# The 32 stores of an instance normalisation go out through GpSimd instead of ScalarE

## The chip, the cores and the metric

The kernel runs on one core of a Trainium2 chip. The metric is the device time of one execution in microseconds (us); the time before is the median of three runs. Within the core, five engines run side by side, each with an instruction stream of its own: TensorE (PE), VectorE (DVE), ScalarE (ACT), GpSimd (POOL) and SyncE (SP). Three of them issue transfers here: SP, ScalarE and GpSimd. Each has a DMA queue of its own, and all queues are served by the same 16 DMA engines.

## The reference

The input x has the shape (4, 8, 16, 256, 256) in float32: 512 channels of 65,536 elements each. Every channel is normalised by its own mean and variance and scaled by one gamma:

```python
mu = x.mean(axis=(3, 4), keepdims=True)
var = ((x - mu) ** 2).mean(axis=(3, 4), keepdims=True)
x_norm = (x - mu) / np.sqrt(var + 1e-5)
out = x_norm * gamma[None, :, :, None, None]
```

So 134.2 MB are read, 134.2 MB are written, and little is computed on each element.

## The kernel before, in words

The work is cut into U = 32 tiles of 128 partitions by 8192 elements, 4 MB each. One channel lies on S = 8 neighbouring partitions, so a tile holds K = 16 channels. In memory a tile is one contiguous block, and a partition's row is 32 KB of it. There are AHEAD = 6 slots in SBUF, `xt0` to `xt5`; tile u uses slot u % 6, and is normalised in place, so that the slot is free for tile u + 6 only when the store of tile u has landed.

The order is written by hand (`manual_schedule`): every engine runs its instructions in the order in which the program names them, and waits are put in where data or a slot are needed. Before the loop, gamma's row of 512 B is loaded on GpSimd's queue (L52), and the first six tiles are loaded (L53 and L54, through the helper at L47 and L48): tiles 1 and 3 on ScalarE's queue, the others on SP's. GpSimd then writes the small constants, among them `navg`, a 128 x 128 block matrix that sums over the eight partitions of a channel and multiplies by -1/65536.

The loop at L100 does the following for each tile:

- L102, VectorE: the sum of each partition's row.
- L103, ScalarE: the sum of the squares of each row; the squares themselves go to a scrap tile.
- L111, TensorE: the matrix `navg` turns both columns into minus the mean and minus the mean square of the channel.
- L112, VectorE, and L116, ScalarE: minus the variance, and its root with 1e-5 added.
- L120 and L122, VectorE: the reciprocal, times gamma.
- L125, VectorE: the whole tile, minus the mean, times the scale, in place.
- L129: the store of the tile, issued by ScalarE.
- L131: the load of tile u + 6 into the slot, issued by SP, which waits for the store of tile u to land.

On ScalarE the order is therefore: squares of tile u (L103), root (L116), store (L129), squares of tile u + 1. The store waits for L125 of its tile, and the next squares stand behind it. On GpSimd nothing is left in the loop. Completion of transfers is counted on semaphores that are handed out in turn, eight for the transfers of SP and ScalarE together and eight for those of GpSimd; a transfer that gets a semaphore again waits until the former user of it has landed.

Of the kernel before, what the change touches and what calls it, by code (L numbers as in the profile page):

```python
# [1 line left out]

# [4 lines left out]

F32 = mybir.dt.float32
U8 = mybir.dt.uint8
ALU = mybir.AluOpType  # L10
ACTF = mybir.ActivationFunctionType
AX = mybir.AxisListType


@with_exitstack
def kernel(
    ctx: ExitStack,
    tc: tile.TileContext,
    x: bass.AP,
    gamma: bass.AP,  # L20
    out: bass.AP,
):
    nc = tc.nc
    B, G, C, H, W = x.shape
    P = nc.NUM_PARTITIONS
    HW = H * W
    n_ch = B * G * C
    S = 8
    K = P // S
    F = HW // S  # L30
    U = n_ch // K
    NG = (G * C) // K
    AHEAD = 6
    assert HW % S == 0 and (G * C) % K == 0

    xv = x.rearrange("b g c h w -> (b g c h w)").rearrange("(u p f) -> u p f", p=P, f=F)
    ov = out.rearrange("b g c h w -> (b g c h w)").rearrange("(u p f) -> u p f", p=P, f=F)
    gv = gamma.rearrange("g c -> (g c)")

    data = ctx.enter_context(tc.tile_pool(name="data", bufs=1))  # L40
    singles = ctx.enter_context(tc.tile_pool(name="singles", bufs=1))
    psum = ctx.enter_context(tc.tile_pool(name="psum", bufs=4, space=bass.MemoryType.PSUM))
    ctx.enter_context(tc.manual_schedule())

    slots = [data.tile([P, F], F32, name=f"xt{i}") for i in range(AHEAD)]

    def load(u, queue):  # L47
        queue.dma_start(out=slots[u % AHEAD][:], in_=xv[u])  # L48


    g_row = singles.tile([1, G * C], F32, name="g_row")
    nc.gpsimd.dma_start(out=g_row[:], in_=gv[None, :])  # L52
    for u in range(AHEAD):  # L53
        load(u, nc.scalar if u in (1, 3) else nc.sync)  # L54


    eps_t = singles.tile([P, 1], F32, name="eps_t")
    nc.gpsimd.memset(eps_t[:], 1e-5)  # L58
    one = singles.tile([1, 1], F32, name="one")
    nc.gpsimd.memset(one[:], 1.0)  # L60
    navg = singles.tile([P, K, S], F32, name="navg")
    nc.gpsimd.memset(navg[:], -1.0 / HW)  # L62
    nc.gpsimd.affine_select(  # L63
        out=navg[:], in_=navg[:], pattern=[[-S, K], [0, S]], compare_op=ALU.is_ge,
        fill=0.0, base=0, channel_multiplier=1,
    )
    nc.gpsimd.affine_select(  # L67
        out=navg[:], in_=navg[:], pattern=[[S, K], [0, S]], compare_op=ALU.is_ge,
        fill=0.0, base=S - 1, channel_multiplier=-1,
    )  # L70
    navg_w = navg[:].rearrange("p k s -> p (k s)")
    root_eps = singles.tile([P, 1], F32, name="root_eps")
    nc.scalar.activation(out=root_eps[:], in_=eps_t[:], func=ACTF.Sqrt)  # L73
    g_rep = singles.tile([1, NG, K, S], F32, name="g_rep")
    g_ps = psum.tile([P, NG], F32, name="g_ps", bufs=1)
    g_col = singles.tile([P, NG], F32, name="g_col")

    nc.vector.tensor_copy(  # L78
        out=g_rep[:],
        in_=g_row[:].rearrange("o (n k) -> o n k", n=NG).unsqueeze(3).to_broadcast([1, NG, K, S]),  # L80
    )
    for n in range(NG):
        nc.tensor.matmul(  # L83
            out=g_ps[:, n : n + 1],
            lhsT=g_rep[:, n].rearrange("o k s -> o (k s)"),
            rhs=one[:],
            start=True, stop=True,
        )
    nc.vector.tensor_copy(out=g_col[:], in_=g_ps[:])  # L89

    junk = singles.tile([P, F], U8, name="junk")

    st = singles.tile([P, U, 2], F32, name="st")
    nvar = singles.tile([P, U], F32, name="nvar")
    std = singles.tile([P, U], F32, name="std")
    rstd = singles.tile([P, U], F32, name="rstd")
    scale = singles.tile([P, U], F32, name="scale")

    squares = []
    for u in range(U):  # L100
        t = slots[u % AHEAD]
        nc.vector.reduce_sum(out=st[:, u, 0:1], in_=t[:], axis=AX.X)  # L102
        square = nc.scalar.activation(  # L103
            out=junk[:], in_=t[:], func=ACTF.Square, accum_out=st[:, u, 1:2],
        )
        if u:

            tc.declare_no_dep(square.ins, squares[-1].ins, reason="junk, ordered by the root between")
        squares.append(square)
        ps = psum.tile([P, 2], F32, name="ps")  # L110
        nc.tensor.matmul(out=ps[:], lhsT=navg_w, rhs=st[:, u], start=True, stop=True)  # L111
        nc.vector.tensor_scalar(  # L112
            out=nvar[:, u : u + 1], in0=ps[:, 0:1], scalar1=ps[:, 0:1],
            scalar2=ps[:, 1:2], op0=ALU.mult, op1=ALU.add,
        )
        nc.scalar.activation(  # L116
            out=std[:, u : u + 1], in_=nvar[:, u : u + 1], func=ACTF.Sqrt,
            bias=eps_t[:], scale=-1.0,
        )
        nc.vector.reciprocal(out=rstd[:, u : u + 1], in_=std[:, u : u + 1])  # L120
        g = u % NG
        nc.vector.tensor_mul(  # L122
            out=scale[:, u : u + 1], in0=rstd[:, u : u + 1], in1=g_col[:, g : g + 1],
        )
        nc.vector.tensor_scalar(  # L125
            out=t[:], in0=t[:], scalar1=ps[:, 0:1], scalar2=scale[:, u : u + 1],
            op0=ALU.add, op1=ALU.mult,
        )
        nc.scalar.dma_start(out=ov[u], in_=t[:])  # L129
        if u + AHEAD < U:  # L130
            load(u + AHEAD, nc.sync)  # L131


# [1 line left out]
_INS = ['x', 'gamma']  # L135
_OUTS = [((4, 8, 16, 256, 256), 'float32')]


# [23 lines left out]
```

## Time and profile before

| what | value |
|---|---|
| time, median of 3 runs (lowest to highest) | 627.16 us (626.78 to 627.45) |
| span of the profiled execution | 625.2 us |
| time around the span (median less span) | 1.96 us |
| VectorE busy | 443.2 us (71%) |
| ScalarE busy | 238.8 us (38%) |
| TensorE matmuls busy | 21.4 us (3%) |
| GpSimd busy | 1.9 us |
| moved by DMA, mean rate | 268.46 MB, 429 GB/s |

The span is that of one profiled execution, from its first to its last record; the profiled execution's own device time is not listed apart, so the median of the runs stands beside it. The page has one line for each engine that divides the span into 40 slices, and a digit in it is the busy share of a slice in tenths, 9 being 90% or more. A line of the groups names the source line, the engine, the operation, what it writes and reads, and how often it runs; behind the first bar stand the total busy time in us and the mean of one in ns, behind the second the idle time of the engine just before these instructions and what ended it. A line of the DMA queues has the packets, the MB and the share of the 16 engines' time. A line of the DMA issues has the size of one in KB and the median time from issue to landing in us. The chain of waits follows the work that ended last back to its start.

### The profile page before, as it was taken

The numbers are of one execution on the slowest core, as the hardware profiler recorded it, in microseconds if no ns is written. First come the engines' busy times: TensorE is split into PE (matmuls) and PEld (weight loads), VectorE is DVE, ScalarE is ACT, GpSimd is POOL, SyncE is SP. The second block draws the span as 40 slices with busy tenths as digits, with TensorE's granted clock in tenths as the row PEclk, the third lists the DMA queues.
The fourth block names the chain that finished last, engine by engine and source line by source line (L and its number), as shares of the span: only waits on it lengthen the run. The fifth ranks groups of instructions, "written<-read, shape, count | busy, mean of one in ns | idle before, by whom it ended". The sixth has DMA issues, their size and how long they took to land.

```text
span 625.2 us, 627 instructions
## 1 busy us (share of the span) xinstructions
PE 21.4 (3%) x80; PEld 19.6 (3%) x80; DVE 443.2 (71%) x162; ACT 238.8 (38%) x98; POOL 1.9 (0%) x10
## 2 busy tenths in 40 slices
PE   2000000000000000000000000000000000000000
PEld 2000000000000000000000000000000000000000
DVE  0588999999776687666786767867668676687730
ACT  0444444444443244432344423444224442244400
POOL 1000000000000000000000000000000000000000
DMA  8999999999999999999999999999999999999998
GB/s 369 436 403 436 436 436 436 436 426 432 434 434 436 424 434 436 436 434 436 436 421 434 434 434 432 432 434 436 436 434 436 436 419 434 434 436 432 432 434 369
DMA packets 9251, 268.46 MB, mean 429 GB/s; under 512 B 1057, under 2 KB 1057, under 8 KB 1057
## 3 DMA queue, kind: packets, MB, share of 16 engines
q10 hardware_dynamic: 4896, 142.61, 52.9%
q1 hardware_dynamic: 4320, 125.83, 46.8%
q14 instruction: 3, 0.02, 0.0%
q0 software_dynamic: 32, 0.00, 0.0%
HBM read 134.22 MB, written 134.22 MB: 429 GB/s over the span
## 4 chain that ended last, share of the span: by engine, by line
another core or an unknown queue 61%; DMA 17%; DVE 15%; SPq 1%; PE 1%; issue 0%; ACT 0%
DMA xt<-in_x_dram 10%; DVE st L102 10%; DMA out_dram<-xt 8%; DVE xt L125 5%; SPq L48 1%; PE ps L111 1%; ACT std L116 0%; DVE nvar L112 0%; DVE rstd L120 0%; DVE scale L122 0%
## 5 line engine op out<-in xcount | busy, mean ns | idle before, releaser
L102 DVE TENSOR_REDUCE st<-xt 128x1 f32<-128x8192 f32 x32 | 277.9, 8684 | 105.3 <-DMA xt<-in_x_dram 105.3
L103 ACT ACTIVATE junk<-xt 128x8192 uint8<-128x8192 f32 x32 | 224.9, 7029 | 275.4 <-DMA xt<-in_x_dram 232.2
L125 DVE TENSOR_SCALAR xt<-xt,ps,scale 128x8192 f32<-128x8192 f32 x32 | 145.6, 4550 | 1.2
L116 ACT ACTIVATE std<-nvar,eps_t 128x1 f32<-128x1 f32 x32 | 9.4, 294 | 79.7 <-DVE nvar L112 79.7
L111 PE MATMUL ps<-st,navg 128*128 128x2 f32 x64 | 17.9, 349 | 562.0 <-DVE st L102 562.0
L111 PEld LDWEIGHTS ps<-st,navg 128*128 128x128 f32 x64 | 16.1, 312 | 563.8 <-issue 563.8
L112 DVE TENSOR_SCALAR nvar<-ps 128x1 f32<-128x1 f32 x32 | 9.2, 287 | 23.9 <-PE ps L111 23.9
L120 DVE RECIPROCAL rstd<-std 128x1 f32<-128x1 f32 x32 | 5.3, 164 | 11.6 <-ACT std L116 11.6
L78 DVE COPY g_rep<-g_row 1x1024 f32<-1x1024 f32 x1 | 0.7, 683 | 10.6 <-DMA g_row<-in_gamma_dram 10.6
L103 ACT ACTIVATION_READ_ACCUMULATOR junk<-xt 128x1 f32 x32 | 6.0, 186 | 0.0
L122 DVE TENSOR_TENSOR scale<-rstd,g_col 128x1 f32<-128x1 f32 x32 | 5.1, 159 | 1.1
L83 PE MATMUL g_ps<-one,g_rep 1*128 1x1 f32 x16 | 3.5, 347 | 11.5 <-DVE g_rep L78 11.5
L83 PEld LDWEIGHTS g_ps<-one,g_rep 1*128 1x128 f32 x16 | 3.5, 326 | 11.4 <-issue 11.4
L89 DVE COPY g_col<-g_ps 128x8 f32<-128x8 f32 x1 | 0.2, 167 | 3.7 <-PE g_ps L83 3.7
L73 ACT ACT_TABLE_LOAD x1 | 1.3, 1283 | 1.7 <-PEq L146 1.7
L52 POOL DMA_DIRECT2D g_row<-in_gamma_dram x1 | 0.6, 607 | 0.8 <-POOLq L146 0.8
L63 POOL TENSOR_SCALAR_AFFINE_SELECT navg<-navg 128x128 f32<-128x128 f32 x1 | 0.4, 398 | 0.1
L67 POOL TENSOR_SCALAR_AFFINE_SELECT navg<-navg 128x128 f32<-128x128 f32 x1 | 0.4, 398 | 0.1
L62 POOL MEMSET navg<- 128x128 f32 x1 | 0.2, 230 | 0.0
L73 ACT ACTIVATE root_eps<-eps_t 128x1 f32<-128x1 f32 x1 | 0.2, 203 | 0.0
L58 POOL MEMSET eps_t<- 128x1 f32 x1 | 0.1, 118 | 0.0
L146 POOL MEMSET const-bfloat16-1.0<- 128x1 bf16 x1 | 0.1, 102 | 0.0
(4 smaller groups left out, 0.4 us busy)
## 6 DMA issues: line engine op xcount, KB each, us to landing
out_dram<-xt ACTq DMA_DIRECT2D x32, 4096.0 KB, 62.5
xt<-in_x_dram SPq DMA_DIRECT2D x30, 4096.0 KB, 38.5
xt<-in_x_dram ACTq DMA_DIRECT2D x2, 4096.0 KB, 31.8
g_row<-in_gamma_dram POOLq DMA_DIRECT2D x1, 0.5 KB, 9.3
```

Of the source, the lines that this page charges most:

```text
L48: queue.dma_start(out=slots[u % AHEAD][:], in_=xv[u])
L73: nc.scalar.activation(out=root_eps[:], in_=eps_t[:], func=ACTF.Sqrt)
L78: nc.vector.tensor_copy(out=g_rep[:], in_=g_row[:].rearrange("o (n k) -> o n k", n=NG).unsqueeze(3).to_broadcast([1, NG, K, S]),)
L83: nc.tensor.matmul(out=g_ps[:, n : n + 1], lhsT=g_rep[:, n].rearrange("o k s -> o (k s)"), rhs=one[:], start=True, stop=True,)
L102: nc.vector.reduce_sum(out=st[:, u, 0:1], in_=t[:], axis=AX.X)
L103: square = nc.scalar.activation(out=junk[:], in_=t[:], func=ACTF.Square, accum_out=st[:, u, 1:2],)
L111: nc.tensor.matmul(out=ps[:], lhsT=navg_w, rhs=st[:, u], start=True, stop=True)
L112: nc.vector.tensor_scalar(out=nvar[:, u : u + 1], in0=ps[:, 0:1], scalar1=ps[:, 0:1], scalar2=ps[:, 1:2], op0=ALU.mult, op1=ALU.add,)
L116: nc.scalar.activation(out=std[:, u : u + 1], in_=nvar[:, u : u + 1], func=ACTF.Sqrt, bias=eps_t[:], scale=-1.0,)
L120: nc.vector.reciprocal(out=rstd[:, u : u + 1], in_=std[:, u : u + 1])
L122: nc.vector.tensor_mul(out=scale[:, u : u + 1], in0=rstd[:, u : u + 1], in1=g_col[:, g : g + 1],)
L125: nc.vector.tensor_scalar(out=t[:], in0=t[:], scalar1=ps[:, 0:1], scalar2=scale[:, u : u + 1], op0=ALU.add, op1=ALU.mult,)
```

## The change

The store at L129 is issued by GpSimd, on GpSimd's own DMA queue, and no longer by ScalarE. All 32 stores move. Nothing else in the program's text changes: the loads, the order of VectorE, TensorE and SP, the slots and the arithmetic stay. Since the semaphores of GpSimd's transfers are a set of their own, loads and stores no longer share one set.

```diff
@@ -126,7 +126,7 @@
             out=t[:], in0=t[:], scalar1=ps[:, 0:1], scalar2=scale[:, u : u + 1],
             op0=ALU.add, op1=ALU.mult,
         )
-        nc.scalar.dma_start(out=ov[u], in_=t[:])
+        nc.gpsimd.dma_start(out=ov[u], in_=t[:])
         if u + AHEAD < U:
             load(u + AHEAD, nc.sync)
```

## The prediction

> **What bounds the kernel now.** I read the page's busy line and its DMA part first, because a kernel that reads and writes 134.2 MB each and computes little should be held by the transfers. From the page of before:
>
> ```profile
> span 625.2 us, 627 instructions
> ...
> DMA  8999999999999999999999999999999999999998
> ...
> q10 hardware_dynamic: 4896, 142.61, 52.9%
> q1 hardware_dynamic: 4320, 125.83, 46.8%
> ...
> q0 software_dynamic: 32, 0.00, 0.0%
> ```
>
> The 16 DMA engines are busy from wall to wall. Queue q1 is SP's (30 loads), q10 ScalarE's (32 stores and 2 loads), q0 GpSimd's (so far only gamma). The shares of the two large queues add up to 99.7%: 623.3 of 625.2 us. So at most 1.9 us of idle DMA time is left in the whole span. The trace's records of single packets say what fills it: 8192 packets of 32,768 bytes (64 DMAs x 128 rows), median 1213 ns. 8192 x 1.213 / 16 = 621.1 us. On each engine the two queues take turns, one packet of q1, then one of q10.
>
> Next I read the groups, to see whether an engine is near that bound.
>
> ```profile
> L102 DVE TENSOR_REDUCE st<-xt 128x1 f32<-128x8192 f32 x32 | 277.9, 8684 | 105.3 <-DMA xt<-in_x_dram 105.3
> L103 ACT ACTIVATE junk<-xt 128x8192 uint8<-128x8192 f32 x32 | 224.9, 7029 | 275.4 <-DMA xt<-in_x_dram 232.2
> L125 DVE TENSOR_SCALAR xt<-xt,ps,scale 128x8192 f32<-128x8192 f32 x32 | 145.6, 4550 | 1.2
> ```
>
> VectorE needs 8.68 + 4.55 + 1.8 for the small steps = 15.05 us a tile; a load and a store take 2 x 9.68 = 19.36 us. VectorE idles 4.35 us a tile on the load. Last, the DMA issues and the end of the chain of waits:
>
> ```profile
> out_dram<-xt ACTq DMA_DIRECT2D x32, 4096.0 KB, 62.5
> xt<-in_x_dram SPq DMA_DIRECT2D x30, 4096.0 KB, 38.5
> ...
> g_row<-in_gamma_dram POOLq DMA_DIRECT2D x1, 0.5 KB, 9.3
> ```
>
> ```profile
> 547.02 38.50 DMA xt<-in_x_dram
> 585.51 0.02 issue
> 585.54 8.70 DVE st L102
> ```
>
> A slot's round is 38.5 (load) + 15.05 (compute) + 62.5 (store) = 116.05 us = 6 slots x 19.36 = 116.2: a store spends 62.5 us on 9.68 us of moving, so the rest is backlog. The last load lands at 585.5, its store is issued at 600.6 and lands with the span's end at 625.2. Of those 24.6 us, 9.7 are its own; 14.9 us is backlog of earlier stores, **the cover of the end**.
>
> **The change, part by part.** Times are against this execution's 625.2 us; the median of the runs shown is 627.16, 1.96 us above it, and I carry that difference over.
>
> *Removed from ScalarE:* 32 DMA issues of 0.338 us = 10.8 us, with the wait of each on L125. ScalarE runs 224.9 + 9.4 + 6.0 us of 625 and idles 275.4 us before L103, of which 232.2 for a load. In the first eight tiles (43.2 us in all) L103 stood behind the store's wait on L125; now it can start earlier, but it takes 7.03 us beside a reduce of 8.68 that can't start earlier, since VectorE itself runs L125 then. Worth 0.
>
> *Added on GpSimd:* 32 issues. GpSimd's other work is 1.90 us, over before the first load lands at 22.8 us, so nothing stands behind a waiting store, and only the next store follows it. Loads on SP wait for the same event as before, the landing of store u. The instruction lists of both programs show SP, VectorE and TensorE in the same order. Semaphores change: a store used to wait for the store four tiles back (77 us earlier, 62.5 to land, so nobody waited); now it waits for that eight back. Worth 0.
>
> *Price of one issue:* the trace has one on this queue, gamma's, 0.607 us, with 32 packets. A store has 144 on its queue now (128 rows, and 16 packets of 4 B that signal the end). Lower bound 0.34 (as ScalarE), upper 0.607 x 144 / 32 = 2.73 us. I take 2.7, the row on the same engine. It delays a store by up to 2.4 us, inside 62.5 us of which 52.8 are backlog: 0 in the middle. At the end 2.4 of the 14.9 us of cover go: 0. Without that cover it would be 2.4 us once, not 32 times.
>
> *GpSimd's issuing beside VectorE.* No row shows an issue of GpSimd beside L125. L125 handles 8192 elements in 4.55 us, L102 the same 8192 in 8.68. A store is issued right after its L125 ends; then VectorE idles 4.35 us and reduces for 8.68, so the next L125 is at least 10.4 us off (8.68 + 1.8, in the first tiles). 2.7 us fit there, so I take 0. Bounds: no clash, or one whole L125, 4.55 us, for a store (backlog again: 0) or the other way 2.7 us for VectorE, inside its 4.35 us of idling. The Trainium skill speaks against this change here: "SBUF — State Buffer", "Who interferes with whom", says that a VectorE instruction in a two-port mode (tensor_scalar can be one, tensor_reduce can't) and a GpSimd instruction block each other until the first ends, and that a DMA issued by GpSimd is starved by it. L125's half time agrees with such a mode; that GpSimd is blocked, no run here shows yet. By that rule alone every store would be up to 4.55 us late, 146 us for 32 if nothing covered them.
>
> *The packets themselves* are the one price no row gives: a 32 KB row on q0. Gamma's 32 packets show that q0 takes turns like the others: its 9 ns packets stand between packets of q1 and q10, and the next packet starts 6 ns later, also after the signalling ones. So turns and signals cost nothing visible. Lower bound of the difference: nothing, 1213 ns is moving time; the whole idle rest, 625.2 - 621.1 = 4.1 us, can't become less than the start of the first load and the last landing, so a gain stays under 1 to 2 us. Upper bound: if rows are cut. The trace has 8192-byte packets of 307 ns; 4 x 307 = 1228, 15 ns above 1213, so about 5 ns a cut. Cut into 4 KB pieces: 7 x 5 to 7 x 9 (the 9 ns of a packet with no data) = 35 to 63 ns a row, x 4096 rows / 16 = 9 to 16 us. I take 0: all 8192 rows here went whole, and gamma's row came as 16 packets of 32 B, one per engine, and 16 of 4 B.
>
> *The end.* For 585.5 to 625.2 us only stores move, on one queue. If that queue had a gap per store, no load would fill it. Lower bound 0 (the 6 ns above); upper bound: the first packets of the kernel took about 1.9 us, 0.7 above 1213; four stores x 0.7 = 2.8 us. I take 0, the nearer row, and keep 2.8.
>
> Sum: 0. 625.2 + 1.96 = 627.2 us.
>
> **Rivals.**
> *A, no change to speak of*, 626.0 to 628.4.
> *B, q0 moves the same bytes at more cost*: rows cut, or gaps with nobody to fill them. For it: q0 has never carried a large row here, and with 99.7% busy every extra ns shows: 4.9 ns a row already make 1.25 us, the point from which it decides. Prices: 2.8 us from the end (630.0), 9 to 16 us for 4 KB pieces (636 to 643).
> *C, stores win the turns from the loads.* Then the last load lands late and the cover is gone. It decides once stores gain more than 14.9 us of moving on the loads, about 1.5 stores; at worst only the last store is left when its load lands, and the end is 15.05 + 9.7 us of bare work after 621.1 - 9.7 us of moving, plus the 4.1 idle: 640. Against it: turns are one packet each now. If the loads win instead, the backlog grows and nothing is lost.
> *D, faster*: store 0 no longer stands behind the two loads on q10, and is in motion some 4 us sooner, at 37.8 us instead of 42. But a full DMA only changes whose packet goes first. At best 1 to 2 us of idle and slow first packets vanish: 625.5.
> *E, the change doesn't act*: the changed program's list has all 32 stores on GpSimd, so it acts; if they still went by q10, 627.2.
>
> **How the numbers follow.** A measurement of this kernel can tell about 0.2% (1.25 us) from no change. A with E 0.50; B 0.35 (a third each near 630, at 636 to 643, and above); C 0.08; D 0.07. Same is A and E, 0.50; slower B and C, 0.43; faster D, 0.07. Predicted time 627.2; its own range 626.0 to 628.4. The 8-in-10 range goes from 625.6 to 641: it leaves out B's third above, the dearest 4 KB pieces and the best of D.
>
> **What would show it.** Right: q0 with 4608 packets and 134 MB and the stores' median time to landing near 60 us; 32 KB packets still near 1213 ns; DMA at 9 in all slices; VectorE still idle about 105 us before L102, L125 at 4550 ns; the last load landing near 585 us. B shows as more packets on q0 or longer ones, and a DMA share over 99% with a longer span, or as gaps in the last 40 us. C shows as shorter stores, longer loads, and a last load after 600 us. A clash with VectorE shows as L125 over 4550 ns or GpSimd issues of more than 4 us. I am wrong above all if a row costs more on this queue.

## The result, and the profile after

The change makes the kernel slower by 0.35%: 628.71 us (median of 8 runs, 628.09 to 632.55) against 627.15 (8 runs), a ratio of 1.0035 with a 95% interval of 1.0025 to 1.0045. The difference of the medians is 1.56 us. That lies in the forecast's range, above the own range of its likeliest case (626.0 to 628.4), and outside what counted there as no change.

The profiled execution of the change took 630.6 us, with a span of 628.6, more than most: six of the eight runs lie between 628.09 and 628.86, two at 630.6 and 632.55. So its trace shows 3.4 us of span more than before, where a usual run has some 1.6. Both have to be explained.

From the page of the change, the lines that answer to those shown of before, and that of the new GpSimd issues (L129):

```profile
span 628.6 us, 628 instructions
...
DMA  8999999999999999999999999999999999999996
...
q0 software_dynamic: 4640, 134.22, 49.5%
q1 hardware_dynamic: 4320, 125.83, 46.6%
q10 hardware_dynamic: 288, 8.39, 3.1%
...
L102 DVE TENSOR_REDUCE st<-xt 128x1 f32<-128x8192 f32 x32 | 277.9, 8683 | 106.4 <-DMA xt<-in_x_dram 106.4
L103 ACT ACTIVATE junk<-xt 128x8192 uint8<-128x8192 f32 x32 | 224.8, 7026 | 235.0 <-DMA xt<-in_x_dram 235.0
L125 DVE TENSOR_SCALAR xt<-xt,ps,scale 128x8192 f32<-128x8192 f32 x32 | 145.6, 4551 | 1.2
L116 ACT ACTIVATE std<-nvar,eps_t 128x1 f32<-128x1 f32 x32 | 9.4, 295 | 121.8 <-DVE nvar L112 121.8
...
L129 POOL DMA_DIRECT2D out_dram<-xt x32 | 17.0, 532 | 582.1 <-DVE xt L125 582.1
...
out_dram<-xt POOLq DMA_DIRECT2D x32, 4096.0 KB, 64.2
xt<-in_x_dram SPq DMA_DIRECT2D x30, 4096.0 KB, 36.4
```

The middle is as before. The stores are on q0 with 4640 - 32 = 4608 packets, rows whole. The trace's single packets of 32 KB have a median of 1213 ns on q0 as on q1. VectorE waits 106.4 us for loads (105.3 before), L125 takes 4551 ns (4550), and the DMA line has its nines. ScalarE's waits only changed their name: its wait on L125 (43.2 us before) is gone, and that of L116 on L112 grew from 79.7 to 121.8 us, by 42.1. What differs is the last digit of the DMA line: 6 after 8. The time went in at the end.

The end stands in the view of line 157, the barrier that closes the program. A line gives shortest, median and longest duration in ns, then the start of the first and of the last. Before:

```profile
L157 POOLq EVENT_SEMAPHORE  x4: 17/17/17, 624.4 to 625.1; - x4
L157 POOLq DRAIN  x3: 40/93/7988, 2.7 to 624.9; - x3
L157 SPq DRAIN  x3: 7/7/7, 624.3 to 624.6; - x3
```

After:

```profile
L157 POOLq EVENT_SEMAPHORE  x4: 17/17/17, 627.8 to 628.5; - x4
L157 POOLq DRAIN  x3: 46/108/25972, 601.8 to 628.3; - x3
L157 SPq DRAIN  x3: 7/7/7, 626.6 to 628.0; - x3
```

SP has seen the last store when its first drain starts, at 624.3 before and 626.6 after. Before, GpSimd is waiting by then and answers at 624.4; its long drain, 7.99 us from 2.7 us on, ended when gamma had landed. After, its drain starts behind the last issue at 601.8, takes 25.97 us and ends at 627.8, **1.2 us after SP knows that everything has landed**. All engines wait for it. By the trace's records of packets and instructions the 3.44 us divide so:

| stretch, us | before | after |
|---|---|---|
| start to first 32 KB packet | 1.81 | 1.82 |
| first to last packet | 622.08 | 624.23 |
| last packet to the end | 1.30 | 2.59 |

The last row is +1.29 us, close to the whole difference of the medians. The middle row, +2.15, is one DMA engine. The last store's last packets end within 0.85 us of each other on 15 engines, and 2.43 us later on the sixteenth. On that engine 26 store packets, one per tile, start right after the load's 4-byte signal and take 1275 to 1354 ns, 2.29 us more than 26 x 1213; on the other engines the signals of load and store follow each other. Before, all 16 end within 1 us.

### The profile page after: what moved, and what is told of

Its sections match the earlier page's. It is cut to its first block, busy times and chain, and to the rows that moved or that the text cites. A ratio compares the mean times of both kernels' runs of the same rounds, so it can differ in the third digit from the quotient of the medians.

```text
span 628.6 us, 628 instructions
## 1 busy us (share of the span) xinstructions
PE 21.4 (3%) x80; PEld 19.5 (3%) x80; DVE 443.2 (71%) x162; ACT 238.1 (38%) x98; POOL 18.9 (3%) x42
## 3 DMA queue, kind: packets, MB, share of 16 engines
q0 software_dynamic: 4640, 134.22, 49.5%
## 4 chain that ended last, share of the span: by engine, by line
another core or an unknown queue 52%; DMA 17%; DVE 15%; issue 10%; SPq 1%; PE 1%; ACT 0%; POOL 0%; POOLq 0%
DVE st L102 10%; DMA xt<-in_x_dram 9%; DMA out_dram<-xt 8%; DVE xt L125 5%; SPq L48 1%; PE ps L111 1%; ACT std L116 0%; DVE nvar L112 0%; POOL out_dram L129 0%; DVE rstd L120 0%; DVE scale L122 0%; POOLq L157 0%; POOLq L129 0%
## 5 line engine op out<-in xcount | busy, mean ns | idle before, releaser
L102 DVE TENSOR_REDUCE st<-xt 128x1 f32<-128x8192 f32 x32 | 277.9, 8683 | 106.4 <-DMA xt<-in_x_dram 106.4
L125 DVE TENSOR_SCALAR xt<-xt,ps,scale 128x8192 f32<-128x8192 f32 x32 | 145.6, 4551 | 1.2
L116 ACT ACTIVATE std<-nvar,eps_t 128x1 f32<-128x1 f32 x32 | 9.4, 295 | 121.8 <-DVE nvar L112 121.8
L129 POOL DMA_DIRECT2D out_dram<-xt x32 | 17.0, 532 | 582.1 <-DVE xt L125 582.1
L112 DVE TENSOR_SCALAR nvar<-ps 128x1 f32<-128x1 f32 x32 | 9.2, 288 | 23.8 <-PE ps L111 23.8
```

The lines of the kernel that those rows point to most:

```text
L112: nc.vector.tensor_scalar(out=nvar[:, u : u + 1], in0=ps[:, 0:1], scalar1=ps[:, 0:1], scalar2=ps[:, 1:2], op0=ALU.mult, op1=ALU.add,)
L116: nc.scalar.activation(out=std[:, u : u + 1], in_=nvar[:, u : u + 1], func=ACTF.Sqrt, bias=eps_t[:], scale=-1.0,)
L125: nc.vector.tensor_scalar(out=t[:], in0=t[:], scalar1=ps[:, 0:1], scalar2=scale[:, u : u + 1], op0=ALU.add, op1=ALU.mult,)
L129: nc.gpsimd.dma_start(out=ov[u], in_=t[:])
```

## The experiments

The theory: (a) GpSimd's drain at the end, (b) one engine out of step. The rival: a price on every store of the queue. Behind each median stand, in brackets, its ratio to the kernel before, timed beside it, and the 95% interval of the ratio.

**1. The last store by ScalarE.**

```diff
-        nc.gpsimd.dma_start(out=ov[u], in_=t[:])
+        (nc.scalar if u == U - 1 else nc.gpsimd).dma_start(out=ov[u], in_=t[:])
```

> Stores 0 to 30 go by GpSimd, the last one by ScalarE. Theory: the 1.6 us of the change have two parts. (a) After its last store GpSimd's drain at the end of the program ends at 627.8 us where the last store had landed at 626.6: 1.2 us, once per kernel, and nothing is left to hide it. (b) On one DMA engine of 16 the turns of loads and stores are out of step, and there the store packet that follows a load's 4-byte signal takes about 1300 instead of 1213 ns, once per tile, 2 us in all in the profiled execution. By (a) this kernel hides the drain behind the last store (9.7 us) and comes to 627.2 to 627.6 us, GpSimd's drain ending well before SP's last wait. Rival: GpSimd's queue costs the same little more on every store; 31 of 32 stores are still there, so 628.6 to 628.8 us.

Measured: 628.77 us (1.0036, 1.0023 to 1.005). That is the rival's number, but the experiment did not do what I meant: the last store, on a queue of its own, took turns with the GpSimd stores still under way, so the two queues ended together, GpSimd's last of all on the one late engine (its last packet 1.2 us after ScalarE's), and the drain was not hidden: 2.56 us from the last packet to the end. It tells nothing apart.

**2. Only the last store by GpSimd.**

```diff
-        nc.scalar.dma_start(out=ov[u], in_=t[:])
+        (nc.gpsimd if u == U - 1 else nc.scalar).dma_start(out=ov[u], in_=t[:])
```

> Only the last store goes by GpSimd, 31 by ScalarE. Theory: part (a) is there in full, since the drain doesn't depend on the number of stores: 1.2 us more than before, 628.3 to 628.5 us, with GpSimd's drain ending about 1.2 us after the last landing. Rival 1, a price per store on GpSimd's queue: 627.2 us. Rival 2, a drain whose time grows with the number of stores issued: under 0.1 us, 627.2 us.

Measured: 627.55 us (1.0009, 1.0000 to 1.0018) against 626.94, between all the theories. The drain ended 0.63 us after its queue's last packet, where the change has 1.74. So this time does depend on what the queue did before.

**3 and 4. All loads by SP, with stores by GpSimd (3) or ScalarE (4).** The edit is the same in both:

```diff
-        load(u, nc.scalar if u in (1, 3) else nc.sync)
+        load(u, nc.sync)
```

> Stores by GpSimd as in the change, and all loads by SP, so that only two queues are in use. The first store then begins in the middle of a load (37.9 us, 3.6 loads after the first byte), and on no engine do the signals of a load and a store follow each other. Theory (b): then on all 16 engines one store packet per tile takes about 85 ns longer, 26 tiles, 2.2 us; with (a) 630.4 to 630.8 us, and 16 packets near 1300 ns per tile. Rival (one engine is slower because of GpSimd's queue, whatever the order of turns): as the change, 628.5 to 628.9 us, one long packet per tile.

> As the kernel before (stores by ScalarE), but all loads by SP, so that here too the first store begins in the middle of a load. Theory (b), if it is a matter of turns and not of the queue that issues: 2.2 us more than before, 629.2 to 629.5 us, with 16 long store packets per tile. Rival, that only GpSimd's queue has it: 627.2 us and no long packets.

Measured: 628.75 us (1.0032, 1.0019 to 1.0045) for 3 and 627.5 us (1.0009, 1.0000 to 1.0018) for 4. My theory of turns falls: in 3 again one engine alone is late, with 26 long packets (2.4 us), not 16 engines; in 4 some ten engines have the signals apart, and no store packet behind a load's signal is long. The rival holds for 3, and a late engine shows only where GpSimd's queue carries the stores.

**5. The last eight stores by ScalarE**, to have GpSimd's drain over early.

```diff
-        nc.gpsimd.dma_start(out=ov[u], in_=t[:])
+        (nc.scalar if u >= U - 8 else nc.gpsimd).dma_start(out=ov[u], in_=t[:])
```

> Stores 0 to 23 by GpSimd, the last eight by ScalarE, so that GpSimd's last store lands more than 30 us before the end and its drain is over by then (sending only the very last store by ScalarE did not do that: in the last 25 us the two queues share the engines and end together). Theory (a), GpSimd's drain is the cost: 627.0 to 627.5 us, no slower than before by more than 0.1%. Rival, the cost lies in the packets of the 24 stores or on the one late engine: 628.2 to 628.6 us. In the profiled execution the late engine should be late by about 1.5 us (18 tiles of 26).

**6. Only the last four stores by GpSimd.**

```diff
-        nc.scalar.dma_start(out=ov[u], in_=t[:])
+        (nc.gpsimd if u >= U - 4 else nc.scalar).dma_start(out=ov[u], in_=t[:])
```

> Only the last four stores by GpSimd. In the change GpSimd's drain ended 1.7 us after the last packet of its queue; with one store there it ended 0.6 us after. Theory A, the drain takes longer the more stores it has issued in the whole program (36 ns each): 0.7 us after the last packet, 627.6 us. Theory B, it depends on how many stores are in flight when it starts (four in the change): 1.7 us after the last packet, 628.4 to 628.8 us.

Measured: 648.72 us (1.0353, 1.0327 to 1.0379) and 646.02 us (1.0302, 1.0287 to 1.0317). Both miss everything that was expected, by 17 to 20 us. From the timeline of the kernel with four GpSimd stores (start, duration, what; in brackets the idle time before and what ended it):

```profile
547.17 8.69 DVE L102 TENSOR_REDUCE st<-xt 128x1 f32<-128x8192 f32 x1 [4.36 <-DMA xt<-in_x_dram]
...
582.12 8.69 DVE L102 TENSOR_REDUCE st<-xt 128x1 f32<-128x8192 f32 x1 [19.92 <-DMA xt<-in_x_dram]
...
616.81 8.69 DVE L102 TENSOR_REDUCE st<-xt 128x1 f32<-128x8192 f32 x1 [19.67 <-DMA xt<-in_x_dram]
...
632.13 0.53 POOL L129 DMA_DIRECT2D out_dram<-xt  x1 [34.16 <-DVE xt L125]
```

The last two tiles wait 19.9 and 19.7 us for their loads, where 4.36 is usual. With the old stores on one queue, the new on a second and the loads on a third, the engines take turns among three, and loads get one turn in three instead of one in two: in the packets of this trace the load, the ScalarE store and the GpSimd store under way at that time end together, each spread over the same 3.7 us. The last load lands at 616.8 instead of 585.5 us, and the last store goes out at 632.1 with no backlog to cover it. This is the prediction's rival C, shown on a kernel that has two store queues at once; the change has one. For the drain they still tell something: in 5 it ended 105 us before the end, and from the last packet to the end it was 1.32 us, as before. In 6 it ended 0.59 us after its queue's last packet; but only the last of the four stores was still under way when it began, so 6 does not tell the number of stores from the number in flight, as it was meant to. Nor does any engine fall behind in 5, where 1.5 us was expected: the signals of a store lie within 1.2 us of each other on the 16 engines up to 449 us, where the change has 4.0 by then.

**7. The stores' issue put beside L125.** GpSimd waits for the scale of the next tile, then issues the store. The load into the slot moves along with it, and the last store follows the loop; both stand outside the lines shown:

```diff
+        if u:
+            nc.gpsimd.tensor_copy(out=gate[:, u : u + 1], in_=scale[:, u : u + 1])
+            nc.gpsimd.dma_start(out=ov[u - 1], in_=slots[(u - 1) % AHEAD][:])
         nc.vector.tensor_scalar(
...
-        nc.gpsimd.dma_start(out=ov[u], in_=t[:])
```

> The store of tile u is held back on GpSimd until the scale of tile u + 1 is ready (a one-column copy on GpSimd waits for it), so that GpSimd issues each store while VectorE runs L125 of the next tile. Theory from the skill's rule on the shared port: the issue of 0.53 us takes until L125 ends, 4 to 5 us, or L125 grows from 4.55 by the issue's 0.5 us. Rival: the two don't meet, 0.53 and 4.55 us stay. The time: a store leaves 15 to 19 us later, out of 43 us of backlog, so less than 1% more by either theory, plus up to 10 us at the end if the last stores have lost their cover.

Measured: 629.4 us (1.0044, 1.0026 to 1.0063). From its groups (L129 is the old L125, L128 the store) and its timeline:

```profile
L129 DVE TENSOR_SCALAR xt<-xt,ps,scale 128x8192 f32<-128x8192 f32 x32 | 145.6, 4551 | 1.2
L128 POOL DMA_DIRECT2D out_dram<-xt x31 | 137.4, 4433 | 1.2
```

```profile
301.32 4.55 DVE L129 TENSOR_SCALAR xt<-xt,ps,scale 128x8192 f32<-128x8192 f32 x1
301.35 0.18 POOL L127 COPY gate<-scale 128x1 f32<-128x1 f32 x1 [14.72 <-DVE scale L123]
301.58 4.41 POOL L128 DMA_DIRECT2D out_dram<-xt  x1
```

An issue that took 0.53 us in the change takes 4.41 here and ends at 305.99, 0.12 us after VectorE's instruction (305.87). VectorE loses nothing. The Trainium skill, "SBUF — State Buffer", "A bandwidth-pool intuition that's wrong (but worth ruling out)", says that a DMA of GpSimd beside a VectorE tensor_copy is blocked until VectorE's end and about 115 ns more: this run agrees, with a tensor_scalar. GpSimd's small copy, which starts 0.03 us after L129, was over in 0.18 us all the same; no run here says why. Yet the time is 0.7 us from the change's, though each of 31 issues lost 3.9 us: the backlog covers it. In this trace no engine was late (all 16 within 1.8 us), though 434 store packets on GpSimd's queue start right after a load's signal, some 16 for a tile: none takes more than 1215 ns. So following a signal is not by itself what makes a packet long. The drain was as in the change (1.87 us after the last packet).

**8 and 9. Two slots instead of six**, with the stores by GpSimd (8) or ScalarE (9).

```diff
-    AHEAD = 6
+    AHEAD = 2
...
-        load(u, nc.scalar if u in (1, 3) else nc.sync)
+        load(u, nc.scalar if u == 1 else nc.sync)
```

> The change with two slots instead of six, so that the backlog of stores which hid GpSimd's issue is gone: a slot's round is load, compute, store, with nothing in between. Theory (the issue of GpSimd is dearer, and only the backlog hid it): slower than the same kernel with ScalarE's stores by 0.5 (issue 0.53 against 0.34 us, and 0.3 us later after L125) to 2.4 us (the prediction's upper price) in each of 16 rounds, 8 to 38 us. Rival (the issue costs nothing even when uncovered): within 2 us of it.

> The kernel before with two slots instead of six, to be set beside the change with two slots. A round of a slot needs at least 9.7 + 15.05 + 9.7 us and two landings, near 38 us, against 38.7 us of DMA work for two tiles: 650 to 720 us. Theory: 8 to 38 us faster than the change with two slots; rival: within 2 us of it.

Measured: 754.8 us with GpSimd (748.7 to 759.4; 1.203 times the kernel before, 1.1965 to 1.2095), 761.6 with ScalarE (760.4 to 762.1; 1.2138, 1.2118 to 1.2158). The theory is wrong in size and sign: without the backlog GpSimd's stores come out 7 us, 0.9%, faster. The 650 to 720 us that I had for the kernel with ScalarE's stores is missed too, by 42 us. The issue lines, GpSimd first:

```profile
out_dram<-xt POOLq DMA_DIRECT2D x32, 4096.0 KB, 15.2
xt<-in_x_dram SPq DMA_DIRECT2D x31, 4096.0 KB, 15.3
```

```profile
out_dram<-xt ACTq DMA_DIRECT2D x32, 4096.0 KB, 16.1
xt<-in_x_dram SPq DMA_DIRECT2D x31, 4096.0 KB, 15.3
```

The store leaves 0.3 us after L125 here (0.03 with ScalarE), but lands 0.9 us sooner after that, in the median. Load and store of the two slots still overlap for part of their way, and how far is set by when each starts. That this overlap is the cause is only argued; it stays open.

**10 to 12. The drain by itself.** The kernel before with small loads of gamma by GpSimd at the start, which nothing uses (n = 31 in 10 and 11, 7 in 12); 11 and 12 also send the last store by GpSimd.

```diff
+    extra = singles.tile([1, n, 16], F32, name="extra")
+    for i in range(n):
+        nc.gpsimd.dma_start(out=extra[:, i], in_=gv[None, 0:16])
...
-        nc.scalar.dma_start(out=ov[u], in_=t[:])
+        (nc.gpsimd if u == U - 1 else nc.scalar).dma_start(out=ov[u], in_=t[:])
```

> The kernel before, its stores on ScalarE, plus 31 loads of 64 B of gamma by GpSimd at the start, which nothing uses. Theory: what the change costs at the end is GpSimd's drain, and it costs only where the queue's last transfer lands at the program's end; here it lands early, so 626.9 to 627.3 us, as before. Rival, every DMA of GpSimd costs a little wherever it is: 628 us and more.

> The same 31 small loads at the start, and the last store by GpSimd: 33 DMAs on its queue as in the change, but only one of them a store. So far the drain ended 0.6 us after its queue's last packet with 2 to 5 DMAs issued, and 1.7 to 1.9 us with 25 to 33, whether one or four were still in flight. Theory A, it depends on how many DMAs the queue was given: 1.7 us after the last packet, the end 2.6 us after it, 628.4 to 628.8 us. Theory B, it depends on the bytes or packets of the stores: 0.6 us and 1.7 us, 627.5 us as with the last store alone.

> Seven small loads at the start and the last store by GpSimd: 9 DMAs on its queue, so that all eight semaphores of the queue are used, as in the change. Theory A with a time that grows per DMA (0.04 us each): drain 0.9 us after the last packet, 627.7 us. Theory A with a step when the semaphores are used a second time: 1.7 us, 628.5 us. Theory B: 0.6 us, 627.5 us.

Measured: 628.08 us (1.0019, 1.001 to 1.0028), 629.51 us (1.0041, 1.0029 to 1.0054) and 628.24 us (1.0021, 1.0012 to 1.003), against 626.8. The small loads are not free, against my expectation, and 628.08 is what the rival had named: from first to last packet 622.98 us in 10, 0.9 more than before, of which their 62 packets on each engine are 0.56 at 9 ns. But 11 has the same 622.98, so the pair 10 and 11 isolates the end: 1.43 us in the medians, 1.45 in the traces. The closing barrier of 10 and then of 11:

```profile
L160 POOLq DRAIN  x3: 40/106/35072, 111.6 to 625.8; - x3
L160 SPq DRAIN  x3: 7/7/7, 625.2 to 625.5; - x3
```

```profile
L160 POOLq DRAIN  x3: 40/99/24961, 601.7 to 627.2; - x3
L160 SPq DRAIN  x3: 7/7/7, 625.5 to 626.9; - x3
```

In 10 the long drain is over at 146.7 us and nobody waits for it. In 11 it ends at 601.7 + 25.0 = 626.7, 1.2 us after SP is ready, as in the change, though one store alone went by GpSimd: the rival, a price on every store, is not needed for this. The drain's time after the last packet, 1.89 us in 11 and 0.91 in 12, is near what a time that grows with the number of DMAs had foretold (1.7 and 0.9); the times are longer than foretold (628.4 to 628.8 and 627.7), as the small loads cost something of their own. The traces whose last packets bear on it:

| kernel | DMAs given to GpSimd | queue's last packet to drain's end, us | last packet of all to the end, us |
|---|---|---|---|
| before | 1 | 0.42, early | 1.30 |
| last store only (2) | 2 | 0.63 | 1.70 |
| last four (6) | 5 | 0.59 | 1.74 |
| 7 small and the last (12) | 9 | 0.91 | 1.75 |
| first 24 (5) | 25 | 1.67 | 1.32 |
| 31 small (10) | 32 | 1.68, early | 1.29 |
| all but the last (1) | 32 | 1.71 | 2.56 |
| the change | 33 | 1.74 | 2.59 |
| two slots (8) | 33 | 1.73 | 2.58 |
| loads by SP (3) | 33 | 1.83 | 2.67 |
| beside L125 (7) | 33 | 1.87 | 2.71 |
| 31 small and the last (11) | 33 | 1.89 | 2.74 |

The third column rises with the number of DMAs that the queue was given, whatever their size, and whether one of its stores was still under way when the drain began (11) or three (the change). Each row is one trace. The drain counts for the time only where GpSimd's last transfer lands at the end.

## Why the prediction was right or wrong, point by point

- **What bounds the kernel** and that the middle can't move: right. 1213 ns a row, 106.4 us of VectorE's waiting, the last load's tile starting at 586.5 us (585.5 before).
- **ScalarE's 32 issues are worth nothing:** right; 43.2 us of one wait came back as 42.1 of another.
- **The issue's price:** I took 2.7 us by scaling with packets; it is 0.531, below gamma's 0.607. An issue of 144 packets costs no more than one of 32. It was hidden all the same. What "uncovered" would cost I had put at up to 2.4 us; with two slots it did not show at all (GpSimd's kernel was the faster one, for a reason left open).
- **No meeting with L125:** right, and for the reason given. Experiment 7 shows that the rule which I weighed against the trace is real; only the place of the issue avoids it.
- **The packets on q0:** whole rows, 1213 ns; taking 0 was right, but for one engine's 2.29 us in the profiled execution. That is rival B's kind, in a form I didn't name. It shows in the three traces of the change and experiments 1 and 3, of executions at 630.5 to 630.6 us, and not in that of experiment 7, at 629.4, nor in that of 5. The six usual runs of the change have spans of 626.1 to 626.9 us; 625.2 and the 1.29 of the end make 626.5, so the 2.15 of a late engine has no room in them if the end costs the same there. No trace of such a run was kept.
- **The end:** the step that failed. I took 0, with 2.8 us kept as an upper bound for gaps between stores. The end did cost 1.29 us, by something not on my list: the wait of GpSimd's own closing drain. The sign was in the view of line 157 of before: a GpSimd drain of 7.99 us for one small load. I had looked at what follows the issue on GpSimd and counted only the next store.
- **Rival C** does not act in the change, but its mechanism is real: two queues of stores at once took the turns from the loads and cost 19 to 21 us.
- **The chances:** the case with 0.50 (no change) did not come true: 628.71 lies above its 628.4, and even the lower end of the interval, 0.25%, is beyond the 0.2% that counted as no change. Slower had 0.43, but for dearer rows, gaps between stores, or lost turns, and none of these is what cost the 1.29 us at the end. That 628.71 lies in the 8-in-10 range is luck: the range went up to 641 for those causes, not for a drain.

No kernel tried here beats the one before.

## What to carry to other kernels

In this kernel, whose DMA engines are full, it mattered little which engine issues the stores, 1.56 us in 627; but two things remained: what the issuing engine has to finish at the program's end, when its last transfer lands last, and in how many queues the transfers of one direction stand, since each queue took a turn. Read the closing barrier in the profile as carefully as the loop. Before a GpSimd issue is put anywhere, look whether a VectorE instruction like L125 runs at that moment; here that made 0.53 us into 4.41.

## What the runs showed of the hardware that I had not expected

- GpSimd's drain ended 0.6 us after its queue's last packet when it had been given 2 to 5 DMAs, 0.9 with 9, 1.7 to 1.9 with 25 to 33. What it does in that time no trace shows.
- With GpSimd's stores one DMA engine of 16 was late in three of the traces, by 1.9 to 2.4 us at the end. The Trainium skill, "DMA: Bandwidth & Descriptors", "Latency and other measured facts", says that engines 7 and 15 are usually slower, and guesses at a cause that only GpSimd's DMAs have. The traces agree that there is a slow engine with this queue alone, but show one, don't number it, and have none in experiments 5 and 7. Why it is late stays open.
- Moving 4 or 24 of the 32 stores to another queue cost more than ten times as much (19 to 21 us) as moving all of them (1.6 us). Moving the last one alone, when no load was left, cost 0.6.
